# One hybrid decoder layer: the weight stream packed by the host, q, k and v computed together per k-tile

## The chip, the cores and the metric

The kernel runs on one core of one Trainium2 chip. Engines: PE (TensorE) multiplies and transposes, PEld is its weight load, DVE is VectorE, ACT is ScalarE, POOL is GpSimd, SP only issues transfers here. The metric is device time in microseconds (us), lower is better; the time of a kernel is the median of its runs. Packing the inputs is done by the host before the launch and is not in the time.

## The reference

One layer with two parallel mixers on 256 positions of width 1024, one batch, all float32. Cut to what matters:

```python
proj = x @ w_in                       # 1024 -> 512 q, 512 k, 512 v, 512 B, 512 C, 512 h, 2048 gates
q, k = partial_rope(q), partial_rope(k)            # first 16 of 64 dims of each of 8 heads
y_att = causal_softmax_attention(q, k, v) @ w_attn_out   # one block of 256: plain causal attention
y_cnv = (B * causal_dwconv3(C * h, conv_w_mix)) @ w_conv_out
g_att, g_cnv = sigmoid(gates + b_gate)             # 1024 each
mix = (g_att * y_att + g_cnv * y_cnv) @ w_o
x = layer_norm(2 ** 0.25 * x + mix, ln1)
u = causal_dwconv3(x @ w_up, conv_w_ffn)           # 1024 -> 5632
f = (silu(u[:, :2816]) * u[:, 2816:]) @ w_down     # 2816 -> 1024
x = layer_norm(2 ** 0.25 * x + f, ln2)
```

## The kernel before

**Three products for one.** Every float32 operand is split into a high part h, rounded to a type that PE takes in one pass, and the rest l = value - h. A product is then h*h + h*l + l*h, three matmuls (`mm3`, L295; `passes`, L465). A split (`hl_split`, L194) is one ACT copy that makes h (L195) and one DVE subtraction that makes l (L196). Both activations and all weights go through it. Below, a *pass* is one matmul with 512 moving columns.

**The weight stream.** All weights, 16.0 million numbers, come from memory in chunks of 1 MB, each of one tile `raw` of 128 x 2048; there are three such tiles (`RAW_BUFS`). The list of chunks is made first: `add_chunk` (L82) notes the transfers of a chunk and its *units*, the pieces that are split at once, two to a chunk, 128 x 1024 numbers each. `issue_dma` (L168) issues, all on SP's queue (L174), the transfers up to two chunks beyond the one whose split begins. A split unit lies in a pair of tiles `wh`, `wl`; there are nine of each (`HL_BUFS`). `ahead(u)` (L323) splits four units (`LA`) beyond the one that PE is about to use. A chunk of w_in or w_up columns is read as 8 x 128 rows of 1 KB, q, k and v chunks as rows of 2 KB, chunks of whole rows of w_o and w_down as rows of 4 KB.

**The order.** The program is in order on each engine, as written. Work that belongs beside the stream is hung on units: `at(u, f)` (L429) puts f after unit u's matmuls, `run(u)` (L432) emits what hangs there.

- *Start.* `warm_up` runs 20 and later 8 matmuls on zeros. x (`xr`, 128 positions on the partitions, two tiles) comes in five pieces between the pieces of the first two chunks. PE transposes it, 16 blocks of 128 x 128 (`x_transpose`, L244), and a split of each result from PSUM gives `xT`: x with the model dimension on the partitions, eight *k-tiles* of 128. Small constants (convolution taps, gate bias) come by five transfers on POOL's queue, as rows; two PE transposes (`small_consts`, L255) and two ACT copies bring them into columns.
- *q, k, v* (L498), one after the other, each over all eight k-tiles, two PSUM banks each (positions 0 to 127 and 128 to 255): 3 x 8 x 2 x 3 = 144 passes. q's first k-tiles are interleaved by hand with the arrival of x (`first_unit`, L473). Rope (`rope`, L337, eight DVE instructions) hangs on the first unit of v, the transposes of q and k (`qk_transpose`) on v's last unit and the first unit after it.
- *conv and gates* (L541 to L571): 12 units of h, C and B and 16 of gates, each 24 matmuls with 256 moving columns (`unit_cols`, L310). Call the first of these units C0 and count from it. Attention hangs on them for four pairs of heads p: `scores` at C0+1+3p, `masked` (mask, maximum; DVE), `exps` (ACT), `normalize` (DVE) one unit later each; `probs_T` (six transposes into two banks) at C0+6+5p, then `probs_hl` twice (split of the probabilities), `attend`, `attend_hl` (split of the attention output; it empties attend's bank).
- *rest*: the output products and gating, w_o, layer norm with x as residual (L624), the FFN with its convolution, w_down, layer norm.

PSUM's eight banks are two rings of four. `acc_bank` holds the accumulators of q, k, v, conv, gates and down; `ps_bank` holds transposes, scores and attend. A bank is given out again in the order of the ring as soon as its last reader is done.

Of the kernel before, what the change touches and what calls it, by code (L numbers as in the profile page):

```python
# [8 lines left out]
F32 = mybir.dt.float32  # L9
# [39 lines left out]

@with_exitstack  # L50
def layer_kernel(ctx: ExitStack, tc: tile.TileContext, x, positions, w_in, b_gate, w_attn_out,
                 conv_w_mix, w_conv_out, w_o, ln1_g, ln1_b, w_up, conv_w_ffn, w_down,
                 ln2_g, ln2_b, out):
    nc = tc.nc
    w_in, w_ao, w_co, w_o, w_up, w_dn = (w[0] for w in (w_in, w_attn_out, w_conv_out, w_o, w_up, w_down))
# [21 lines left out]
    WARM = (20, 8)  # L77
    units = []
    dmas = []
    state = {"dma": 0}  # L80

    def add_chunk(loads, views):  # L82

        c = len(dmas)
        dmas.append(dict(loads=loads, tile=None))
        for v in views:
            units.append(dict(chunk=c, view=v, h=None, l=None))

    def kxn(w, k0, k1, c0, c1):
        return w[k0 * P:k1 * P, c0:c1].rearrange("(k p) n -> p k n", p=P)  # L90

    def chunk_cols(w, c0, order=None):
        add_chunk([(lambda t: t.rearrange("p (k n) -> p k n", k=8), kxn(w, 0, 8, c0, c0 + 256))],
                  [(lambda t, u=u: t.rearrange("p (k n) -> p k n", k=8)[:, :, u * P:(u + 1) * P], [8, P])
                   for u in range(2)] if order is None else order)

    U = {}

    def mark(name):
        U[name] = len(units)  # L100


    def x_load(k0, k1):
        return (lambda t: xr[:, :, k0 * P:k1 * P], x[0, :, k0 * P:k1 * P].rearrange("(t p) d -> p t d", p=P))

    def k_load(c, k0, k1):
        return (lambda t: t.rearrange("p (k n) -> p k n", k=4)[:, k0:k1, :],
                kxn(w_in, c * 4 + k0, c * 4 + k1, 0, 512))

    for i, nm in enumerate("qkv"):  # L110
        mark(nm)
        for half in range(2):
            loads = [(lambda t: t.rearrange("p (k n) -> p k n", k=4),
                      kxn(w_in, half * 4, half * 4 + 4, i * 512, i * 512 + 512))]
            if i == 0 and half == 0:
                loads = [x_load(0, 1), k_load(0, 0, 1), x_load(1, 2), k_load(0, 1, 2), x_load(2, 4), k_load(0, 2, 3), k_load(0, 3, 4)]
            elif i == 0:
                loads = [x_load(4, 6), k_load(1, 0, 1), k_load(1, 1, 2), x_load(6, 8), k_load(1, 2, 4)]
            add_chunk(loads, [(lambda t, u=u: t.rearrange("p (k n) -> p k n", k=4)[:, 2 * u:2 * u + 2, :], [2, 512])
                              for u in range(2)])  # L120

    OFF_B, OFF_C, OFF_H, OFF_G = 3 * AW, 3 * AW + CW, 3 * AW + 2 * CW, 3 * AW + 3 * CW
    for pr in range(2):
        for off in (OFF_H, OFF_C, OFF_B):
            U[(off, pr)] = len(units)
            chunk_cols(w_in, off + pr * 256)
    for pr in range(8):
        U[("g", pr)] = len(units)
        chunk_cols(w_in, OFF_G + pr * 256)

    for half in range(2):
        for nm, w in (("ao", w_ao), ("co", w_co)):
            U[(nm, half)] = len(units)
            add_chunk([(lambda t: t.rearrange("p (k n) -> p k n", k=4), kxn(w, 0, 4, half * 512, half * 512 + 512))],
                      [(lambda t, u=u: t.rearrange("p (k n) -> p k n", k=4)[:, :, u * 256:(u + 1) * 256], [4, 256])
                       for u in range(2)])

    def row_chunk(w, k):
        add_chunk([(lambda t: t.rearrange("p (k n) -> p k n", k=2), kxn(w, k, k + 2, 0, D))],
                  [(lambda t, u=u: t.rearrange("p (k n) -> p k n", k=2)[:, u:u + 1, :], [1, D]) for u in range(2)])  # L140

    mark("wo")
    for k in range(0, 8, 2):
        row_chunk(w_o, k)

    mark("up0")
    for half in range(2):
        add_chunk([(lambda t: t.rearrange("p (k n) -> p k n", k=4)[:, :, 0:256], kxn(w_up, half * 4, half * 4 + 4, 0, 256)),
                   (lambda t: t.rearrange("p (k n) -> p k n", k=4)[:, :, 256:512],
                    kxn(w_up, half * 4, half * 4 + 4, DFF, DFF + 256))],  # L150
                  [(lambda t, u=u: t.rearrange("p (k n) -> p k n", k=4)[:, 2 * u:2 * u + 2, :], [2, 512])
                   for u in range(2)])
    TAIL = 8
    for c in range(1, NP // 2):
        U[("ug", c)] = len(units)
        chunk_cols(w_up, c * 256)
        U[("uv", c)] = len(units)
        chunk_cols(w_up, DFF + c * 256)
        d = c - 2
        if 0 <= 2 * d < NP - TAIL:  # L160
            U[("dn", d)] = len(units)
            row_chunk(w_dn, 2 * d)
    for d in range((NP - TAIL) // 2, NP // 2):
        if ("dn", d) not in U:
            U[("dn", d)] = len(units)
            row_chunk(w_dn, 2 * d)

    def issue_dma(c):  # L168
        while state["dma"] <= c and state["dma"] < len(dmas):
            d = dmas[state["dma"]]  # L170
            t = wp.tile([P, 2048], F32, tag="raw", name=f"raw{state['dma']}", bufs=RAW_BUFS)
            d["tile"] = t
            for fn, src in d["loads"]:
                nc.sync.dma_start(fn(t), src)  # L174
            state["dma"] += 1

    def split_start(u):
        un = units[u]
        issue_dma(un["chunk"] + RAW_BUFS - 1)
        k, n = un["view"][1]  # L180
        un["h"] = wp.tile([P, k, n], F32R, tag="wh", name=f"wh{u}", bufs=HL_BUFS)
        un["l"] = wp.tile([P, k, n], F32R, tag="wl", name=f"wl{u}", bufs=HL_BUFS)

    def split_part(u, k0, k1, eng=None):
        un = units[u]
        src = un["view"][0](dmas[un["chunk"]]["tile"])
        hl_split(un["h"][:, k0:k1], un["l"][:, k0:k1], src[:, k0:k1], eng)

    def split(u, eng=None):
        if u < len(units) and units[u]["h"] is None:  # L190
            split_start(u)
            split_part(u, 0, units[u]["view"][1][0], eng)
# [18 lines left out]

    warm_up(WARM[0])

# [16 lines left out]
    nc.gpsimd.dma_start(posi, positions[0].rearrange("(t p) -> p t", p=P))  # L230
    rowsA = cst.tile([116, P], F32, name="rowsA")
    cf = conv_w_ffn[0].rearrange("t (j p) -> t j p", p=P)
    nc.gpsimd.dma_start(rowsA[0:44], cf[0])
    nc.gpsimd.dma_start(rowsA[44:88], cf[1])
    nc.gpsimd.dma_start(rowsA[88:104], b_gate[0].rearrange("(j p) -> j p", p=P))
    nc.gpsimd.dma_start(rowsA[104:116], conv_w_mix[0].rearrange("t (j p) -> (t j) p", p=P))
    rowsB = cst.tile([44, P], F32, name="rowsB")
    nc.gpsimd.dma_start(rowsB, cf[2])
# [5 lines left out]
    def x_transpose(k0, k1):  # L244
        b = ps_bank(f"xt{k0}")
        for k in range(k0, k1):
            for t in range(2):
                nc.tensor.transpose(b[:, (k - k0) * 256 + t * P:(k - k0) * 256 + (t + 1) * P],
                                    xr[:, t, k * P:(k + 1) * P], ident)
        hl_split(xh[:, k0:k1, :], xl[:, k0:k1, :], b[:, 0:(k1 - k0) * 256].rearrange("p (j t) -> p j t", j=k1 - k0))  # L250

    cA = cst.tile([P, 116], F32, name="cA")
    cB = cst.tile([P, 44], F32, name="cB")

    def small_consts():  # L255
        b = ps_bank("cst")
        nc.tensor.transpose(b[:, 0:116], rowsA, ident[:116, :116])
        nc.tensor.transpose(b[:, 128:172], rowsB, ident[:44, :44])
        nc.scalar.activation(cA, b[:, 0:116], AF.Copy)
        nc.scalar.activation(cB, b[:, 128:172], AF.Copy)  # L260

    def w_ffn(tap, j):
        return cB[:, j:j + 1] if tap == 2 else cA[:, tap * 44 + j:tap * 44 + j + 1]

    def bias_gate(j):
        return cA[:, 88 + j:89 + j]

    def w_mix(tap, j):
        return cA[:, 104 + tap * 4 + j:105 + tap * 4 + j]
# [31 lines left out]
    def unit_rows(u, k0, banks, ah, al, first, last, ts=(0, 1)):  # L301

        un = units[u]
        nk = un["view"][1][0]
# [5 lines left out]
    def unit_cols(u, o, bh, bl, n0=0):  # L310

        un = units[u]
        nk = un["view"][1][0]
# [137 lines left out]
    C0 = U[(OFF_H, 0)]  # L451
    for p in range(4):
        s = C0 + 1 + 3 * p
# [434 lines left out]
```

## Time and profile before

| | |
|---|---|
| time, median of 3 runs | 380.79 us (379.37, 381.06, 380.79) |
| the profiled execution | 378.92 us, of which its span 377.1 us |
| granted PE clock, mean over the span | 0.993 |
| stages on PE, from the chain | q to 19.8, k to 30.9, v to 41.8, conv and gates from there |
| DMA | 68.65 MB, mean 182 GB/s over the span |
| SP's queue | 66.07 MB in 48992 packets |

The span runs from the first to the last instruction. A row of the timeline has start, duration, engine, line, operation, output <- input and count, with the idle time before it and who ended it in brackets. A row of the chain has start, duration, engine, output, line and count. A row of waits has the waiting engine and line, whom it waited for, the total, the count and the longest. A row of groups has the shape, the count, the busy time and the mean ns of one, then the idle time before. A row of windows has the stretch, its length, the busy time and count of PE, PEld, DVE, ACT and POOL, then granted clock, DMA share and GB/s. A row of transfers has the count, the size in units of 1024 bytes and the us to landing. A matmul's duration contains its pipeline: matmuls follow each other faster than they last.

### The profile page before, as it was taken

How to read it: one execution, taken by the hardware profiler on the slowest of the kernel's cores; microseconds unless marked ns; L12 is line 12 of the kernel's file. 1: busy time of each engine (PE TensorE's matmuls, PEld its weight loads, DVE VectorE, ACT ScalarE, POOL GpSimd, SP SyncE). 2: the span in 40 equal slices, each digit the busy share in tenths (PEclk: the TensorE clock that was granted, in tenths of full speed). 3: DMA queues.
4: the chain of work that ended last, by engine and by line, in shares of the span. 5: the costliest groups of instructions: out<-in, count | busy, mean ns of one | idle time of the engine just before them, and what ended most of it. 6: DMA issues, size and time to landing. Idle time of an engine off the chain costs nothing.

```text
span 377.1 us, 6375 instructions
## 1 busy us (share of the span) xinstructions
PE 367.1 (97%) x2582; PEld 342.4 (91%) x2582; DVE 273.1 (72%) x455; ACT 200.5 (53%) x325; POOL 12.6 (3%) x33
## 2 busy tenths in 40 slices
PE   7999999999999999999999999999999999999991
PEld 6888999999999999988899999999999999999891
DVE  2777777778536458879879876958769687678584
ACT  4667485648655545544167563646546555466200
POOL 5000000000000000102100000000000000000012
PEclk9999999999999999999999999999999999999997
DMA  7996764444644445497451919365493765660011
GB/s 214 370 320 216 227 197 139 130 139 164 211 139 159 177 143 194 140 345 245 163 196 43 314 28 312 114 224 175 160 318 106 249 220 170 228 237 38 2 56 56
DMA packets 49789, 68.65 MB, mean 182 GB/s; under 512 B 1431, under 2 KB 40032, under 8 KB 49760
## 3 DMA queue, kind: packets, MB, share of 16 engines
q1 hardware_dynamic: 48992, 66.07, 51.9%
q0 software_dynamic: 768, 2.18, 1.7%
q8 instruction: 20, 0.33, 0.4%
q14 instruction: 9, 0.07, 0.1%
HBM read 67.19 MB, written 1.05 MB: 181 GB/s over the span
## 4 chain that ended last, share of the span: by engine, by line
PE 96%; DMA 1%; DVE 1%; SPq 0%; issue 0%; DVEq 0%
PE pb L318 10%; PE pb L317 10%; PE pb L316 10%; PE d L298 5%; PE d L297 5%; PE d L299 5%; PE g L317 4%; PE g L316 4%; PE g L318 4%; PE q L470 3%; PE y L318 2%; PE y L317 2%; PE y L316 2%; PE o L297 2%; PE o L299 2%; PE o L298 2%
## 5 line engine op out<-in xcount | busy, mean ns | idle before, releaser
L196 DVE TENSOR_TENSOR wl<-raw,wh 128x1024 fp32r<-128x1024 f32 (+1 forms) x126 | 148.2, 1188 | 55.3 <-ACT wh L195 53.4
L195 ACT ACTIVATE wh<-raw 128x1024 fp32r<-128x1024 f32 (+1 forms) x126 | 127.1, 1025 | 48.8 <-DMA raw<-in_w_up 33.1
L316 PE MATMUL pb<-x1T,wh 128*128 128x256 f32 x320 | 90.6, 283 | 0.0
L318 PE MATMUL pb<-x1T,wl 128*128 128x256 f32 x320 | 90.6, 283 | 0.0
L317 PE MATMUL pb<-x1T,wh 128*128 128x256 f32 x320 | 90.5, 283 | 0.0
L317 PEld LDWEIGHTS pb<-x1T,wh 128*128 128x128 f32 x320 | 61.4, 192 | 0.6
L316 PEld LDWEIGHTS pb<-x1T,wh 128*128 128x128 f32 x320 | 61.4, 192 | 0.6
L318 PEld LDWEIGHTS pb<-x1T,wl 128*128 128x128 f32 x320 | 61.4, 192 | 0.0
L316 PE MATMUL g<-xT,wh 128*128 128x256 f32 x128 | 36.5, 285 | 0.0
L318 PE MATMUL g<-xT,wl 128*128 128x256 f32 x128 | 36.2, 283 | 0.0
L317 PE MATMUL g<-xT,wh 128*128 128x256 f32 x128 | 36.2, 283 | 0.0
L297 PE MATMUL d<-wh,f 128*128 128x512 f32 x80 | 31.3, 391 | 0.0
L298 PE MATMUL d<-wl,f 128*128 128x512 f32 x80 | 31.3, 391 | 0.0
L299 PE MATMUL d<-wh,f 128*128 128x512 f32 x80 | 31.1, 389 | 0.0
L694 DVE SCALAR_TENSOR_TENSOR fc<-pb,cA,fc 128x255 f32<-128x255 f32 x44 | 21.0, 477 | 7.2 <-ACT fc L690 7.2
L317 PEld LDWEIGHTS g<-xT,wh 128*128 128x128 f32 x128 | 24.5, 192 | 0.0
L316 PEld LDWEIGHTS g<-xT,wh 128*128 128x128 f32 x128 | 24.5, 192 | 0.0
L318 PEld LDWEIGHTS g<-xT,wl 128*128 128x128 f32 x128 | 24.5, 192 | 0.0
L690 ACT ACTIVATE fc<-pb,cB 128x256 f32<-128x256 f32 x44 | 18.2, 464 | 10.2 <-PE pb L318 8.4
L696 DVE SCALAR_TENSOR_TENSOR fc<-pb,cA,fc 128x254 f32<-128x254 f32 x44 | 21.2, 482 | 1.6
L299 PEld LDWEIGHTS d<-wh,f 128*128 128x128 f32 x80 | 15.0, 188 | 3.2
L297 PEld LDWEIGHTS d<-wh,f 128*128 128x128 f32 x80 | 15.1, 188 | 2.7
(193 smaller groups left out, 665.8 us busy)
## 6 DMA issues: line engine op xcount, KB each, us to landing
raw<-in_w_up SPq DMA_DIRECT2D x20, 1024.0 KB, 5.6
raw<-in_w_in SPq DMA_DIRECT2D x18, 1024.0 KB, 5.2
raw<-in_w_down SPq DMA_DIRECT2D x11, 1024.0 KB, 6.9
raw<-in_w_o SPq DMA_DIRECT2D x4, 1024.0 KB, 4.8
raw<-in_w_attn_out SPq DMA_DIRECT2D x2, 1024.0 KB, 4.9
raw<-in_w_conv_out SPq DMA_DIRECT2D x2, 1024.0 KB, 4.8
raw<-in_w_up SPq DMA_DIRECT2D x4, 512.0 KB, 6.5
raw<-in_w_in SPq DMA_DIRECT2D x6, 256.0 KB, 5.5
```

Source lines behind the costliest of these rows:

```text
L195: nc.scalar.activation(h, src, AF.Copy)
L196: (eng or nc.vector).tensor_tensor(l, src, h.bitcast(F32), op=ALU.subtract)
L297: nc.tensor.matmul(o, ah, bh, start=start, stop=False)
L298: nc.tensor.matmul(o, ah, bl, start=False, stop=False)
L299: nc.tensor.matmul(o, al, bh, start=False, stop=stop)
L316: nc.tensor.matmul(o, wh, bh[:, k, :], start=k == 0, stop=False)
L317: nc.tensor.matmul(o, wh, bl[:, k, :], start=False, stop=False)
L318: nc.tensor.matmul(o, wl, bh[:, k, :], start=False, stop=k == nk - 1)
L470: nc.tensor.matmul(banks[t], x2[p == 2], un["l" if p == 1 else "h"][:, k, :], start=start and p == 0, stop=stop and p == 2)
L690: nc.scalar.activation(c, pb[:, a * S:(a + 1) * S], AF.Copy, scale=w_ffn(2, j))
L694: nc.vector.scalar_tensor_tensor(c[:, 1:S], pb[:, a * S:a * S + S - 1], w_ffn(1, j), c[:, 1:S], op0=ALU.mult, op1=ALU.add)
L696: nc.vector.scalar_tensor_tensor(c[:, 2:S], pb[:, a * S:a * S + S - 2], w_ffn(0, j), c[:, 2:S], op0=ALU.mult, op1=ALU.add)
```

## The change

The host packs all weights, and x transposed, into one array `wpack` of chunks x 128 x 2048 in the order of use (`packed`, `plan`), so that a chunk of 1 MB is 128 rows of 8 KB. The first eight chunks are new: chunk k holds k-tile k of x transposed (256 columns), of w_in's q and k columns (1024, one unit) and of its v columns (512, one unit), 1792 columns or 917 KB. Chunks behind these have the same contents and the same split units as before. `cpack` is the small constants in columns, 128 x 160.

- x_transpose, small_consts and their copies and splits go; x comes split from `raw` (`x_split`), the constants come by one transfer.
- q, k and v are computed k-tile by k-tile (`qkv_passes`): per k-tile 18 passes into six banks, v's two from `ps_bank`.
- Chunk 0 comes in four pieces (x on ACT's queue, q, k and v on SP's), chunk 1 in two, all others in one.
- k-tile 0 is split in part on DVE alone (x and the q half: copy and subtraction), the rest on ACT and DVE. All later k-tiles are split two k-tiles ahead.
- 36 warm-ups in one group, in place of 20 and 8.
- The first four conv units are split during k-tiles 6 and 7.
- Rope moves behind C0, qk_transpose behind C0+2 and C0+3, scores to C0+4+3p, probs_T to C0+9+4p, the rest with them. Conv and gates stay.
- x for the residual (`xr`, 1 MB) comes in one transfer on SP's queue behind chunk 20.

The core of the diff:

```diff
+    mark("qkv")
+    for k in range(KT):
+        chunk((1, S, [("xT", k, k + 1, 0, S)]),
+              (2, 512, [("w_in", k, k + 1, 0, 1024)]),
+              (1, 512, [("w_in", k, k + 1, 1024, 1536)]))
...
+    PIECES = {0: (0, 256, 768, 1280, 1792), 1: (0, 768, 1792)}
+    XR_CHUNK = 20
     def issue_dma(c):
...
+            cuts = PIECES.get(i, (0, end))
+            for a, b in zip(cuts, cuts[1:]):
+                (nc.scalar if i == b - 256 == 0 else nc.sync).dma_start(t[:, a:b], wpack[i, :, a:b])
+            if i == XR_CHUNK:
+                nc.sync.dma_start(xr, x[0].rearrange("(t p) d -> p t d", p=P))
...
-    warm_up(WARM[0])
+    warm_up(36)
...
+    consts = cst.tile([P, 160], F32, name="consts")
+    nc.gpsimd.dma_start(consts, cpack)
...
-    at(3, small_consts)
-    at(5, rope_tables)
-    at(U["v"], rope, 0)
-    at(U["v"], rope, 1)
+    at(C0, rope, 0)
+    at(C0, rope, 1)
     for i, g2 in enumerate((0, 2, 1, 3)):
-        at(U["v"] + 3 + i // 2, qk_transpose, g2)
+        at(C0 + 2 + i // 2, qk_transpose, g2)
     for p in range(4):
-        s = C0 + 1 + 3 * p
+        s = C0 + 4 + 3 * p
...
-        s = C0 + 6 + 5 * p
+        s = C0 + 9 + 4 * p
...
+    def x_split(k):
+        issue_dma(k + RAW_BUFS - 1)
+        hl_split(xh[:, k, :], xl[:, k, :], raws[k][:, 0:S])
+    def qkv_split(k):
+        if k < KT:
+            x_split(k)
+            split(U["qkv"] + 3 * k + 1)
+            split(U["qkv"] + 3 * k + 2)
...
+    banks = [[acc_bank(f"{m}{t}") for t in range(2)] for m in "qk"] + [[ps_bank(f"v{t}") for t in range(2)]]
+    def qkv_passes(k, m, ts, ps):
+        wh, wl = qkv_weights(k, m)
+        for t in ts:
+            for p in ps:
+                nc.tensor.matmul(banks[m][t], (xl if p == 2 else xh)[:, k, t * P:(t + 1) * P], wl if p == 1 else wh,
+                                 start=k == 0 and p == 0, stop=k == KT - 1 and p == 2)
+    split_start(1)
+    issue_dma(RAW_BUFS - 1)
+    nc.vector.tensor_copy(xh[:, 0, :], raws[0][:, 0:S])
+    nc.vector.tensor_tensor(xl[:, 0, :], raws[0][:, 0:S], xh[:, 0, :].bitcast(F32), op=ALU.subtract)
+    w0, wh0, wl0 = raw_of(1), units[1]["h"], units[1]["l"]
+    nc.vector.tensor_copy(wh0[:, 0], w0[:, 0])
+    qkv_passes(0, 0, (0, 1), (0, 2))
+    nc.vector.tensor_tensor(wl0[:, 0], w0[:, 0], wh0[:, 0].bitcast(F32), op=ALU.subtract)
+    qkv_passes(0, 0, (0, 1), (1,))
+    split_part(1, 1, 2)
+    qkv_passes(0, 1, (0, 1), (0, 2, 1))
+    split(2)
+    qkv_passes(0, 2, (0, 1), (0, 2, 1))
+    qkv_split(1)
+    qkv_split(2)
+    for k in range(1, KT):
+        for m in range(3):
+            if k >= KT - 2 and m < 2:
+                split(C0 + 2 * (k - KT + 2) + m)
+            qkv_passes(k, m, (0, 1), (0, 1, 2))
+            if k == KT - 1:
+                if m < 2:
+                    evac_rows(m, banks[m])
+                else:
+                    evac_v(banks[m])
+        qkv_split(k + 2)
+        if k == 2:
+            rope_tables()
+    cur["u"] = C0 + 4
```

More of the change, by code (lines that the diff above doesn't have):

```diff
@@ L50, in layer_kernel @@
 @with_exitstack
-def layer_kernel(ctx: ExitStack, tc: tile.TileContext, x, positions, w_in, b_gate, w_attn_out,
-                 conv_w_mix, w_conv_out, w_o, ln1_g, ln1_b, w_up, conv_w_ffn, w_down,
-                 ln2_g, ln2_b, out):
+def layer_kernel(ctx: ExitStack, tc: tile.TileContext, x, positions, wpack, cpack, ln1_g, ln1_b, ln2_g, ln2_b, out):
     nc = tc.nc
-    w_in, w_ao, w_co, w_o, w_up, w_dn = (w[0] for w in (w_in, w_attn_out, w_conv_out, w_o, w_up, w_down))
     cst = ctx.enter_context(tc.tile_pool(name="cst", bufs=1))
@@ L76, in layer_kernel @@
     RAW_BUFS, HL_BUFS = 3, 9
[L77 to L166, printed above, removed]
-    def issue_dma(c):
[L169 to L175, printed above, removed]
+    chunks, plan_units, U = plan()
@@ new lines, in layer_kernel @@
+    units = [dict(chunk=c, off=off, shape=(k, n), h=None, l=None) for c, off, k, n, _ in plan_units]
+    raws = []
+    PIECES = {0: (0, 256, 768, 1280, 1792), 1: (0, 768, 1792)}
+    XR_CHUNK = 20
+    def issue_dma(c):
+        while len(raws) <= c and len(raws) < len(chunks):
+            i = len(raws)
+            t = wp.tile([P, CHUNK], F32, tag="raw", name=f"raw{i}", bufs=RAW_BUFS)
+            raws.append(t)
+            last = units[chunks[i][-1]]
+            end = last["off"] + last["shape"][0] * last["shape"][1]
+            cuts = PIECES.get(i, (0, end))
[3 more added lines that the diff above has]
+                nc.sync.dma_start(xr, x[0].rearrange("(t p) d -> p t d", p=P))
@@ L179, in split_start, with raw_of @@
         issue_dma(un["chunk"] + RAW_BUFS - 1)
-        k, n = un["view"][1]
+        k, n = un["shape"]
         un["h"] = wp.tile([P, k, n], F32R, tag="wh", name=f"wh{u}", bufs=HL_BUFS)
         un["l"] = wp.tile([P, k, n], F32R, tag="wl", name=f"wl{u}", bufs=HL_BUFS)
+    def raw_of(u):
+        un = units[u]
+        k, n = un["shape"]
+        return raws[un["chunk"]][:, un["off"]:un["off"] + k * n].rearrange("p (k n) -> p k n", k=k)
     def split_part(u, k0, k1, eng=None):
         un = units[u]
-        src = un["view"][0](dmas[un["chunk"]]["tile"])
-        hl_split(un["h"][:, k0:k1], un["l"][:, k0:k1], src[:, k0:k1], eng)
+        hl_split(un["h"][:, k0:k1], un["l"][:, k0:k1], raw_of(u)[:, k0:k1], eng)
     def split(u, eng=None):
@@ L191, in split @@
             split_start(u)
-            split_part(u, 0, units[u]["view"][1][0], eng)
+            split_part(u, 0, units[u]["shape"][0], eng)
     def hl_split(h, l, src, eng=None):
@@ L303, in unit_rows @@
         un = units[u]
-        nk = un["view"][1][0]
+        nk = un["shape"][0]
         for t in ts:
@@ L463, in layer_kernel, with qkv_weights @@
         at(s + 4, attend_hl, p)
-    def passes(c, k, banks, ts, ps, start=False, stop=False):
-        un = units[c]
+    def x_split(k):
[6 more added lines that the diff above has]
+            split(U["qkv"] + 3 * k + 2)
+    def qkv_weights(k, m):
+        ua, ub = (units[U["qkv"] + 3 * k + 1 + e] for e in range(2))
+        return (ub["h"][:, 0, :], ub["l"][:, 0, :]) if m == 2 else (ua["h"][:, m, :], ua["l"][:, m, :])
```

154 lines of the change are left out of this document (78 added, 76 removed).

## The prediction

> **What bounds the kernel now.** I read the busy table and the heads of the chain first.
>
> ```profile
> span 377.1 us, 6375 instructions
> PE 367.1 (97%) x2582; PEld 342.4 (91%) x2582; DVE 273.1 (72%) x455; ACT 200.5 (53%) x325; POOL 12.6 (3%) x33
> PE 96%; DMA 1%; DVE 1%; SPq 0%; issue 0%; DVEq 0%
> ```
>
> PE is the bound, on 96% of the chain. The view of waits, for PE alone, has only three rows, and I set one row of ACT's beside them:
>
> ```profile
> PE warm L210 <- DVE zeros L200: 1.0, 1, 1.0
> PE xt L248 <- DMA xr<-in_x: 0.8, 1, 0.8
> PE q L470 <- ACT wh L195: 0.5, 1, 0.5
> ACT wh L195 <- DMA raw<-in_w_up: 33.1, 16, 3.4
> ```
>
> All three of PE's waits lie in the first 8 us. ACT waits 33.1 us for streamed weights in the FFN, yet none of this reaches PE: the splits run four units ahead. So time can come from two places only, work taken off PE and the start. The chain in order of time shows the start:
>
> ```profile
> 7.86 0.66 PE xt L248 x4
> 8.52 1.84 PE q L470 x8
> 10.36 0.50 PE xt L248 x4
> 10.86 2.76 PE q L470 x12
> 13.62 0.44 PE xt L248 x4
> 14.05 5.50 PE q L470 x24
> 19.84 0.43 PE k L297
> ...
> 41.83 0.87 PE qkt L354 x8
> ```
>
> From 7.86 us on PE never stops. The k and v stages are 96 passes (matmuls of 512 columns) between 19.84 and 41.83, so 0.229 us for one. Of q's 48 passes 8 + 12 + 24 = 44 stand behind 7.86, so 140 passes of q, k and v: 140 x 0.229 = 32.07. Between them lie 12 of the 16 transposes of x (0.66 + 0.50 + 0.44 = 1.60) and, from 19.55 to 19.84, the two transposes of the constants (0.29). 7.86 + 32.07 + 1.60 + 0.29 = 41.82: the stage is accounted for. Its end, 41.83, is what I predict anew. After it PE has the same matmuls in both kernels.
>
> **The change, part by part.**
>
> *Transposes gone.* The 12 on the chain and the two of the constants: 1.60 + 0.29 = 1.89 us of PE, off the path. The other four lie in the start, which is reckoned anew.
>
> *The first k-tile.* It needs the warm-ups, x's first piece and the q piece. For these and the next step:
>
> ```profile
> 0.74 0.43 SPq L174 DMA_DIRECT2D xr<-in_x  x1
> 0.99 2.05 PEld L210 LDWEIGHTS <-zeros 128*128 128x128 bf16 x20 [0.99 <-DVE zeros L200]
> 1.24 0.45 SPq L174 DMA_DIRECT2D raw<-in_w_in  x1
> 4.36 0.63 ACT L195 ACTIVATE wh<-raw 128x512 fp32r<-128x512 f32 x1 [0.21 <-DMA raw<-in_w_in]
> 5.04 1.22 PE L470 MATMUL q<-wh,xT 128*128 128x512 f32 x2 [0.46 <-ACT wh L195]
> 2.00:8.00 6.00, 4.78 (x30) 3.72 (x28) 1.84 (x4) 2.04 (x5) 4.11 (x17) 1.00 0.91 251
> 8.00:12.00 4.00, 4.00 (x22) 3.26 (x22) 2.76 (x5) 2.75 (x6) 0.00 (x0) 1.00 1.03 353
> 2.00:3.00 1.00, 1.00 (x13) 1.00 (x10) 0.00 (x0) 0.03 (x1) 0.99 (x12) 1.00 0.97 216
> 3.00:4.00 1.00, 1.00 (x10) 0.93 (x9) 0.00 (x0) 0.23 (x1) 1.00 (x2) 1.00 0.94 311
> L196 DVE TENSOR_TENSOR wl<-raw,wh 128x1024 fp32r<-128x1024 f32 x13 | 15.4, 1222 | 4.9 <-ACT wh L195 4.8
> L195 ACT ACTIVATE wh<-raw 128x1024 fp32r<-128x1024 f32 x13 | 13.0, 1054 | 2.4 <-DMA raw<-in_w_in 2.4
> L196 DVE TENSOR_TENSOR wl<-raw,wh 128x512 fp32r<-128x512 f32 x8 | 5.2, 686 | 0.6 <-ACT wh L195 0.6
> L195 ACT ACTIVATE wh<-raw 128x512 fp32r<-128x512 f32 x8 | 4.7, 625 | 0.2 <-DMA raw<-in_w_in 0.2
> L196 DVE TENSOR_TENSOR xT<-xt,xT 128x256 fp32r<-128x256 f32 x2 | 0.8, 425 | 4.6 <-ACT xT L195 4.6
> L195 ACT ACTIVATE xT<-xt 128x256 fp32r<-128x256 f32 x2 | 0.8, 384 | 3.4 <-PE xt L248 3.4
> ```
>
> The 36 warm-ups at 2.05 / 20 = 0.103 us run from 0.99 to 4.7; I put 4.8. The old first weight piece, 262 KB, was issued at 1.24 and read at 4.36, so 3.1 us; the q piece, the same size and first on its queue at 0.74, is due by 3.9, and x's 131 KB on ACT's queue sooner. A DVE copy of 512 has no row: at most the subtraction's 0.69, at least the 0.42 of half the length. So the first weights are ready at 4.3 to 4.6, behind the warm-ups. First pass: 4.8, against 5.04. The two passes at 5.04 took 1.22, 0.6 each, where settled ones are 0.229 apart; with the first three at 0.4 and 15 at 0.229 the 18 passes of k-tile 0 end at 4.8 + 1.2 + 3.4 = 9.4.
>
> *The second k-tile.* New and decisive: its q and k weights are one unit of 1024 columns, split by one ACT instruction that waits for both pieces of chunk 1. Ahead of that landing the queues carry 131 + 3 x 262 + 393 + 524 = 1835 KB and 82 KB of constants, 1917 KB. Slow bound: the old kernel's own pace, 16 KB by 2 us, then 251 GB/s to 8 us (1506 KB) and 353 for the other 395 KB: 9.1 us. Fast bound: 353 GB/s from 2.0 on: 7.4. I take 216 and 311 GB/s for 2 to 4 us, then 353, so 4 + (1917 - 16 - 527) / 353 = 7.9, because the old queue mixed x's short rows and five small POOL transfers into 4 to 8 us, while the new pieces are rows of 2 KB and more. With 0.2 until ACT starts: wh from 8.1 to 9.15 (1054 ns), wl to 10.4 (1222 ns). The second pass of k-tile 1 needs wl, so PE waits from about 9.6 to 10.4. From there 125 of the 144 passes are left: 10.4 + 125 x 0.229 = 39.0. k-tile 2 is 917 KB behind: at 353 GB/s 2.6 us later, 10.7, split by 0.38 + 1.05 + 1.22 at about 13.6, and PE arrives at 10.4 + 17 x 0.229 = 14.3. Each later one gains 4.1 - 2.6 us.
>
> Term one: 41.83 - 39.0 = **2.8 us less** (1.89 of transposes, 0.9 of start); bounds 9.1 and 7.4 us for the landing give 1.6 and 3.3.
>
> *Six banks.* v's two come from the other pool; q and k are emptied while v's passes run (6 x 0.229 = 1.4 us against two copies near 0.6). Nothing.
>
> *Conv units split early.* Four splits of 1.05 and 1.22 move into k-tiles 6 and 7, where 18 passes take 4.1 us and ACT has 0.38 + 1.05 + 0.63 of its own. Nothing; without that cover, 1.2 us at the first conv unit.
>
> *Rope and attention later.* Rope, eight DVE instructions, sits behind v's two subtractions and one split, its reader three units later. Scores, softmax and transposes of probabilities follow three units later than before, and after the first pair at a step of 4, not 5. Here a wait is new. The score banks of pair 3 (the scores now stand right behind attend_hl(0) and probs_T(1)) include the bank that attend(0) filled, so the second matmul of these scores waits until DVE has emptied it; everything on PE stands behind. Before, that bank went to the next transposes, a unit later. Rows:
>
> ```profile
> 50.20 0.32 PE c L316
> 59.03 0.89 PE s L369 x12
> L532 DVE SCALAR_TENSOR_TENSOR ct<-z,cA,ct 128x256 f32<-128x256 f32 x8 | 3.7, 482 | 0.1
> L196 DVE TENSOR_TENSOR aT<-av,aT 64x256 fp32r<-64x256 f32 x8 | 3.4, 422 | 6.6 <-ACT aT L195 6.4
> L377 DVE CUSTOM_DVE_ANT_0 sm<-s,mask 128x256 f32<-128x256 f32 x8 | 3.1, 421 | 0.0
> L377 DVE CUSTOM_DVE_ANT_0 sm<-s,mask 128x128 f32<-128x128 f32 x8 | 2.0, 287 | 1.2 <-PE s L369 1.2
> 80.00:85.00 5.00, 5.00 (x48) 4.79 (x47) 4.86 (x18) 2.46 (x6) 0.00 (x0) 1.00 0.34 97
> ```
>
> Three units take 59.03 - 50.20 = 8.83 us. From the end of scores(2) PE needs 8.83, attend's 1.0 (3 x 0.23 + 3 x 0.12) and six transposes (0.87 / 8 each, 0.65): 10.5 us. DVE meanwhile: mask 1.4 (2 x 0.42 + 2 x 0.29), conv taps 4 x 0.48, a split 1.22, the product 0.69, yT 0.63 (ACT) and 0.69, a split 1.22, twice aT 0.38 (ACT) and 0.42: 9.4 us, and 2.6 us in front (z 0.69, a split 1.22, vpt at most 0.69) as far as not done earlier. So between 1.1 us of slack and 1.5 us of wait; I take 0.2 of wait, the middle. The order of gates and exponentials also costs ACT two more table loads; gate banks are needed again four units, 11.8 us, later. Nothing.
>
> *Stream laid out by the host, x late.* Rows of 1 KB become 8 KB. The issues by line show what row length does:
>
> ```profile
> raw<-in_w_in SPq DMA_DIRECT2D x18, 1024.0 KB, 5.2
> raw<-in_w_down SPq DMA_DIRECT2D x11, 1024.0 KB, 6.9
> ```
>
> w_down's rows of 4 KB land in 6.9 us, the w_in chunks, mostly rows of 1 KB, in 5.2: no gain from length, and no wait of PE's to shorten. x's 1 MB now goes into SP's queue behind chunk 20, during the gates; the chunk behind it comes some 3 us later (1049 KB at 353), covered by splits 11.8 us ahead. Without cover, 3 us. The four POOL transfers fewer are worth nothing beyond the start.
>
> A rule of the Trainium skill goes further ("DMA: Bandwidth & Descriptors", Rules for kernel authors: for full bandwidth, 128 partitions and at least 1 MiB per transfer, small ones merged). By it larger transfers would be worth something wherever data is awaited, here at the start alone; the two rows above, both of 1 MB, cannot show it.
>
> **Sum.** 2.8 - 0.2 = 2.6 us less, span 374.5. The profiled execution took 378.92 (span 377.1 and 1.82 around it), 1.87 below the median of the runs, 380.79; with its own surroundings it would be 376.3. Against the median: **378.2 us**; its own range, from the landing, 377.6 to 379.0.
>
> **The rivals.**
>
> *The start is slow as before* (21%). If 251 GB/s belongs to the first microseconds and not to the short rows, chunk 1 lands at 9.1, wl is ready at 11.6 and the stage ends at 40.2: gain 1.6 - 0.2 = 1.4, 379.4 us. For it: 4.78 of 6 us PE busy and DMA at a share of 0.91 in that row, so the engines were not idle. Against: 311 GB/s at 3 to 4 us.
>
> *The stream is at full pace at once* (10%). Landing at 7.4, wl at 9.9, end 38.5, no ring wait: gain 3.3, 377.5 us. The Trainium skill's rule above leans this way. Against: 216 GB/s at 2 to 3 us with 2 KB rows already among them.
>
> *The bank wait decides* (11%, slower). One place: pair 3's scores behind attend_hl(0). If DVE is a further 3.5 us late when it comes to the mask of pair 2, the wait is 1.5 + 3.5 = 5.0, and 380.79 - 2.8 + 5.0 = 383.0 us. It ends above the old time from a wait of 2.8 us on. For it: DVE at 4.86 of 5 us in 80 to 85, and the attention now denser. Against: PE is at 5.00 in that same row, and DVE has spare time before.
>
> *The host's layout brings nothing*: already in the sum, at zero.
>
> **How the numbers follow.** A measurement of this kernel cannot tell less than about 0.5%, 1.9 us, from no change (its runs lie 1.7 apart); the line for faster is 378.9. Forecast 58%, of which 5 points end above that line. Faster: 53 + 10 = 63%. Same: 5 + 21 = 26%. Slower: 11%. Range 376.7 to 380.5: the fast start less 0.8 of scatter, the slow start with nearly the whole 1.5 of bank wait in place of 0.2, 1.1 more.
>
> **What would show it.** In the changed kernel's profile: no matmuls of x's transposes; first q pass near 4.8; one PE wait on k-tile 1's weights, near 0.8 us, ended by ACT's wh or DVE's wl; the first conv matmul near 39.0; a PE wait of at most 1.5 us at pair 3's scores; no other wait of PE's; PE rates of 0.229 and 2.94 / 24 us unchanged. Wrong would be: waits at k-tile 2 or later, a wait for raw during the FFN, or a longer matmul step.

## The result and the profile after

| | before | changed |
|---|---|---|
| median of 5 runs | 380.79 us (379.37 to 381.83) | 377.76 us (377.59 to 377.95) |
| ratio of the runs | 1 | 0.9945 (95% interval 0.9923 to 0.9967) |
| profiled execution, span | 378.92, 377.1 | 377.95, 376.2 |
| first matmul after v, start | 41.67 us | 40.45 us |

The changed kernel is faster by 0.55% by this ratio and by 0.80% by the two medians: the ratio is not formed from the medians, whose quotient, 377.76 / 380.79, is 0.9920. Three figures do not fit together with one cause: the medians lie 3.0 us apart, the two profiled executions only 1.0, and the old runs are spread over 2.5 us, the new ones over 0.4. Most of the experiments are about that.

The page of the changed kernel begins:

```profile
span 376.2 us, 6359 instructions
PE 366.5 (97%) x2572; PEld 342.6 (91%) x2572; DVE 273.7 (73%) x461; ACT 203.4 (54%) x327; POOL 10.3 (3%) x29
```

PE is still the bound. Its waits (waiting engine and line, whom it waited for, total, count, longest) are two, where there were three:

```profile
PE warm L202 <- DVE zeros L192: 1.0, 1, 1.0
PE q L451 <- DVE wh L460: 0.6, 1, 0.6
```

So nothing behind the first pass waited in this execution, neither at k-tile 1 nor at the scores of pair 3. The chain in order of time (start, duration, what) shows the start:

```profile
0.74 3.71 DMA raw<-in_wpack
4.47 0.30 DVE xT L457
4.80 0.43 DVE xT L458
5.22 0.35 DVE wh L460
5.61 2.93 PE q L451 x6
8.54 2.13 PE k L451 x6
10.67 1.38 PE v L451 x6
12.05 1.36 PE q L451 x6
...
39.25 1.36 PE v L451 x6
```

These rows show two rates of the same instruction. From 12.05 on six passes take 1.36 us, 0.227 each, as later everywhere. The first six took 2.93 and the next 2.13: k-tile 0 took 6.44 us instead of 4.08. And x, issued at 0.74, was read at 4.47, 1.5 us after the old kernel's first piece of the same size (issued at 0.74, read at 3.00). The timeline shows when k-tile 1 was ready (start, duration, engine, line, operation, count, idle time before):

```profile
9.07 1.58 ACT L187 ACTIVATE wh<-raw 128x1024 fp32r<-128x1024 f32 x2 [1.13 <-DMA raw<-in_wpack]
...
10.16 1.83 DVE L188 TENSOR_TENSOR wl<-raw,wh 128x1024 fp32r<-128x1024 f32 x2 [1.76 <-ACT wh L187]
```

Chunk 1's second piece was read at 9.07, and with 1.2 us for its subtraction wl was ready at 11.4. PE came at 11.9, late enough by its own slowness not to wait. Everything behind follows 1.2 us earlier than before: the first matmul after v starts at 40.45 instead of 41.67, and the last DVE instruction at 371.61 instead of 372.84. Between these two points both kernels take the same time, 331.16 and 331.17 us, so in the two profiles the whole gain lies in the start. Of the 1.23, 0.3 is lost after the last DVE instruction, where only the output transfers are left; what they waited for was not tried.

### The profile page after: what moved, and what is told of

Its sections match the earlier page's. It is cut to its first block, busy times and chain, and to the rows that moved or that the text cites. A ratio compares the mean times of both kernels' runs of the same rounds, so it can differ in the third digit from the quotient of the medians.

```text
span 376.2 us, 6359 instructions
## 1 busy us (share of the span) xinstructions
PE 366.5 (97%) x2572; PEld 342.6 (91%) x2572; DVE 273.7 (73%) x461; ACT 203.4 (54%) x327; POOL 10.3 (3%) x29
## 4 chain that ended last, share of the span: by engine, by line
PE 96%; DVE 1%; DMA 1%; issue 0%; DVEq 0%
PE pb L286 10%; PE pb L285 10%; PE pb L284 10%; PE d L265 5%; PE d L266 5%; PE d L267 5%; PE g L284 4%; PE g L286 4%; PE g L285 4%; PE q L451 3%; PE k L451 3%; PE v L451 3%; PE y L286 2%; PE y L285 2%; PE y L284 2%; PE o L266 2%
## 5 line engine op out<-in xcount | busy, mean ns | idle before, releaser
L188 DVE TENSOR_TENSOR wl<-raw,wh 128x1024 fp32r<-128x1024 f32 (+1 forms) x126 | 147.5, 1183 | 50.3 <-ACT wh L187 47.8
L187 ACT ACTIVATE wh<-raw 128x1024 fp32r<-128x1024 f32 (+1 forms) x126 | 126.9, 1023 | 43.3 <-DMA raw<-in_wpack 34.9
L665 DVE SCALAR_TENSOR_TENSOR fc<-pb,consts,fc 128x255 f32<-128x255 f32 x44 | 20.9, 476 | 13.9 <-ACT fc L661 13.9
L661 ACT ACTIVATE fc<-pb,consts 128x256 f32<-128x256 f32 x44 | 18.3, 468 | 18.5 <-PE pb L286 16.6
L667 DVE SCALAR_TENSOR_TENSOR fc<-pb,consts,fc 128x254 f32<-128x254 f32 x44 | 21.2, 481 | 1.6
```

The source lines that it names most:

```text
L187: nc.scalar.activation(h, src, AF.Copy)
L188: (eng or nc.vector).tensor_tensor(l, src, h.bitcast(F32), op=ALU.subtract)
L661: nc.scalar.activation(c, pb[:, a * S:(a + 1) * S], AF.Copy, scale=w_ffn(2, j))
L665: nc.vector.scalar_tensor_tensor(c[:, 1:S], pb[:, a * S:a * S + S - 1], w_ffn(1, j), c[:, 1:S], op0=ALU.mult, op1=ALU.add)
L667: nc.vector.scalar_tensor_tensor(c[:, 2:S], pb[:, a * S:a * S + S - 2], w_ffn(0, j), c[:, 2:S], op0=ALU.mult, op1=ALU.add)
```

## The experiments

All were run against the kernel before on the same chip. Each has 5 to 12 runs, and those of the kernel before, 30, 17 and 18 on three chips, have medians of 379.8, 380.2 and 379.8 us. All of these lie below the 380.79 of the five runs above.

**The kernel before once more** (no edit).

> The kernel before, unchanged, to see how much of the 3.0 us between the two medians (380.79 and 377.76) lies in its own scatter: its first profile had a span of 377.1, only 0.9 above the changed kernel's 376.2. Theory 'path' (the start of the old kernel is the same each time): this profile again ends v at 41.8 and has a span of 376.8 to 377.5. Rival 'moving start' (the moment from which a 512-column pass takes 0.23 us instead of 0.43, and the landings of x, differ from execution to execution): v ends 0.5 to 2.5 us elsewhere, with the difference all before 15 us, and the times spread over 2 us again while the changed kernel's spread over 0.4.

379.28 us median (378.88 to 382.64, 12 runs); the profiled execution, 380.91, had a span of 379.1, and the first matmul after v started at 43.66, 2.0 later than in its first profile. One of PE's waits:

```profile
PE xt L248 <- DMA xr<-in_x: 2.2, 1, 2.2
```

and PE's timeline behind it:

```profile
8.53 1.12 PE L248 MATMUL xt<-ident,xr 128*128 128x128 f32 x4 [2.22 <-DMA xr<-in_x]
...
9.88 1.05 PE L470 MATMUL q<-wh,xT 128*128 128x512 f32 x2
...
11.79 0.40 PE L470 MATMUL q<-wl,xT 128*128 128x512 f32 x1
```

The wait for x's third piece was 2.2 us in place of 0.8, and after it passes ran 0.42 apart until about 11.6. The windows (length, busy times, then granted clock, DMA share, GB/s) name the reason:

```profile
9.00:10.00 1.00, 1.00 (x6) 0.90 (x5) 0.00 (x0) 0.31 (x1) 0.00 (x0) 0.50 1.09 400
10.00:11.00 1.00, 1.00 (x4) 0.81 (x3) 0.68 (x2) 1.00 (x3) 0.00 (x0) 0.50 1.05 384
```

The granted clock was 0.50. "Moving start" held: the old kernel loses time twice in such an execution, by the late piece and by the half clock behind the gap. The Trainium skill ("TensorE: Matmul & The Clock Gate", Part 1: The HAM clock gate) puts such a fall to half rate after at least one idle window of some 3.4 us, and says that the windows run free. The trace agrees in the half, 0.50, and in a fall during an idle stretch, but this stretch was 2.2 us, shorter than the page's window; here the measurement decides.

**Filling that wait.** The granted clock may fall because PE is idle, or the late piece alone may matter.

```diff
             passes(c, 0, banks, (0,), (1, 2))
+            warm_up(16)
             x_transpose(2, 4)
```

> The kernel before with 16 warm-up matmuls more, just ahead of the transposes that wait for x's third piece; the granted clock fell to 0.50 in its second profile after a wait of 2.2 us there, and passes ran 0.42 apart until 11.6. Theory 'gap' (the clock falls because PE is idle): with the wait filled the runs above 380.5 become rare, the best runs stay at 378.8 to 379.6 (the filling costs up to 0.9 us where x is on time), mean clock 0.99 or more in every run. Rival 'only the landing' (x is late, the clock is a side effect): the scatter to 381 and 382 stays.

Runs in order, us and mean granted clock of the span:

```
before, same chip: 378.67 .994  379.19 .996  379.32 .996  379.35 .996  379.43 .996  379.49 .993  379.50 .997  379.51 .994  379.74 .992
                   379.91 .995  380.05 .996  380.75 .988  380.79 .988  381.02 .988  381.09 .988  381.09 .989  381.11 .989  382.23 .986
filled:            378.82 .993  379.03 .994  379.05 .994  379.25 .996  379.27 .996  379.27 .996  379.42 .996  379.46 .993  379.97 .994
                   380.31 .995  380.41 .995  380.58 .995
```

"Gap" held. Unfilled, 7 of 18 runs lie at 380.7 or above, each with a mean clock below 0.99; filled, no run of 12 has such a clock and one reaches 380.5. The profiled execution, at 380.31 one of the slower ones, shows a full clock where 0.50 had been granted:

```profile
9.00:10.00 1.00, 1.00 (x11) 1.00 (x9) 0.00 (x0) 0.00 (x0) 0.00 (x0) 1.00 1.06 390
```

Median 379.35 against 379.83, ratio 0.9988 (0.9972 to 1.0004): what is won in the bad runs is not enough to be certain in the median, but no run of that class was seen again. The class is a part of the old median that one profile alone does not show. It is not all of the scatter: on the other two chips 14 of 47 runs of the kernel before have such a clock, but six more lie at 380.9 to 382.2 with a clock of 0.992 to 0.994. No trace of such a run was taken, and what slows them stays open.

**The transposes alone.** x transposed and the constants in columns come from the host; x for the residual is therefore loaded later, and nothing else changes.

```diff
-                nc.tensor.transpose(b[:, (k - k0) * 256 + t * P:(k - k0) * 256 + (t + 1) * P],
-                                    xr[:, t, k * P:(k + 1) * P], ident)
-        hl_split(xh[:, k0:k1, :], xl[:, k0:k1, :], b[:, 0:(k1 - k0) * 256].rearrange("p (j t) -> p j t", j=k1 - k0))
+        hl_split(xh[:, k0:k1, :], xl[:, k0:k1, :], xraw[:, k0:k1, :])
...
-    at(3, small_consts)
```

> The kernel before with one part of the change alone: x transposed and the constants in columns come from the host, so that PE's 18 transposes and their five PSUM splits go; x for the residual is loaded later. Order of q, k, v, pieces, warm-ups and attention stay. Theory 'path': the 12 transposes on the chain (1.60) and the two of the constants (0.29) fall away and q's start keeps its waits for data: the stage ends 1.9 to 2.5 us earlier than 41.8, so nearly the whole gain of the change is here. Rival 'start decides' (the first passes wait for data and run slowly, so that work taken off PE turns into waiting): less than 1 us.

378.56 us (378.12 to 379.50, 12 runs), ratio 0.9958 (0.9939 to 0.9976): 1.2 us less in the median, 0.7 in the best run, and no run above 379.5. Its profiled execution (379.06, not one of its best) has these waits of PE:

```profile
PE q L452 <- ACT wh L199: 2.8, 3, 1.3
PE q L452 <- DVE wl L200: 0.4, 2, 0.2
```

The median lies between the two theories, as "path" asked for 1.9 to 2.5 us and "start decides" for less than 1; the best run goes with the second. In this execution the 1.89 us of transposes on PE became waiting. PE waited 3.2 us for q's weights, in five places up to 11.66, where the old profile has 0.8 and 0.5 behind the warm-ups, and the first matmul after v started at 41.87, no earlier than before. The median won all the same, and the scatter is gone already here: no run of 12 has a mean clock below 0.993.

In that order q alone asks for 393 KB (x and weights) per 6 passes, 1.36 us of PE, which is 289 GB/s, when the old kernel's queues moved, from 2 to 8 us, 251 and 233 GB/s in its two profiles and 223 here (the changed kernel's 315). Six banks ask for 917 KB per 18 passes, 4.08 us: 225 GB/s. This is a reason to expect something of the order by k-tiles, but that order was not run alone. The changed kernel lies 0.7 to 0.8 us below this run's median, on other chips, and the order shares that with the warm-ups, the pieces and the later attention.

**The layout alone.** All chunks contiguous in memory, with the pieces, the order and the transposes as before.

```diff
-        dmas.append(dict(loads=loads, tile=None))
+        dmas.append(dict(loads=loads if c < 2 else [(lambda t: t, wpack[c])], tile=None))
...
-        return (lambda t: t.rearrange("p (k n) -> p k n", k=4)[:, k0:k1, :],
-                kxn(w_in, c * 4 + k0, c * 4 + k1, 0, 512))
+        return (lambda t: t[:, k0 * 512:k1 * 512], wpack[c, :, k0 * 512:k1 * 512])
```

> The kernel before with the host's layout alone: every chunk's tile is 128 contiguous rows of 8 KB in memory; the same units, pieces of the first two chunks, order and transposes. Theory 'nobody waits for the stream' (after 8 us PE never waits): best run within 0.4 us of the kernel before's best, 378.8, median within 0.6, and scatter as before. Rival 'the stream's layout is worth something': 1 us or more less, in the best run as in the median. In between: the start's pieces land sooner and the scatter shrinks.

380.29 us (379.59 to 380.94, 12 runs) against 380.23, ratio 0.9999 (0.9981 to 1.0017). Nothing in the median, as reckoned. The scatter was narrower on both sides, and the best run was 0.6 us worse than the other's best, 378.97, where at most 0.4 had been expected; in the profiled execution q's first weights were read at 4.97 instead of 4.36. Why is not known.

**x early.** `XR_CHUNK = 20` becomes 2.

> The changed kernel with x for the residual (1 MB) behind chunk 2 instead of chunk 20, so ahead of chunk 3 on SP's queue. Chunk 3 and those after it land 2.5 to 3 us later (1.05 MB at 350 to 420 GB/s). In the changed kernel k-tile 3 is read at 13.4 and reached by PE at 20.2, with 2.7 us of splitting between: 4 us of spare time. Theory 'covered': the same time within 0.3 us. Rival 'x late is part of the gain' (the stream has no such reserve in the first 20 us): PE waits at k-tile 3 or 4 and 0.5 to 3 us are lost.

377.72 us (377.55 to 378.15, 6 runs); the changed kernel itself on that chip took 377.84. "Covered" held: a megabyte ahead of chunk 3 costs nothing.

**The changed kernel once more** (no edit).

> The changed kernel, unchanged, beside the variants on the same chip. 'Steady start' (it reaches its first weights late and runs them slowly, but without a gap of PE's behind them): 377.5 to 378.0 in all runs, first pass 5.4 to 5.8, fast steps of 0.227 from 9 to 10 us, the kernel before scattered from 378.8 to 382. 'Chance' (the few runs seen were alike by accident): times up to 379 or more.

377.84 us (377.38 to 378.19, 6 runs), ratio 0.9927 (0.9899 to 0.9955). The narrow spread held, a little wider than the 377.5 to 378.0 expected, but the reason given for it did not. This execution started quickly:

```profile
5.69 1.21 PE L451 MATMUL q<-wh,xT 128*128 128x512 f32 x4 [1.02 <-DVE wh L460]
...
10.40 0.50 PE L451 MATMUL q<-wh,xT 128*128 128x512 f32 x1 [0.30 <-ACT wh L187]
...
11.66 0.50 PE L451 MATMUL q<-wl,xT 128*128 128x512 f32 x1 [0.76 <-DVE wl L188]
```

Four passes took 1.21 us instead of 2.08; PE then reached k-tile 1 at 10.1 and waited 1.06 us for it. The first matmul after v started at 40.14, against 40.45. So the changed kernel has two bounds that lie close together: slow passes until 9.6, or wl of k-tile 1 at 11.3 to 11.7. Whichever of the two ways an execution started, it ended within 0.3 us of the other (spans 376.2 and 375.9).

**More warm-ups.** `warm_up(36)` becomes 44.

> The changed kernel with 44 warm-ups in place of 36, which at 0.107 us each end near 5.7 instead of 4.8 and so cover the 0.6 us in which PE waits for the first weights. In the changed kernel the first 9 passes start 0.43 us apart, until about 9.6, instead of 0.227. Theory 'activity' (PE is slow until it has been busy without a gap for long enough): the fast steps begin 1 to 3 us earlier, k-tile 0 ends near 10.5 instead of 12.05, k-tile 1 then waits for wl (ready near 11.4), and the stage ends 0.5 to 0.9 us earlier. Rival 'fixed moment' (the fast steps begin at a moment that does not hang on the gap): they begin at 9.6 again, or anywhere, and the time is the same within 0.3 us. Trainium skill, 'TensorE: Matmul & The Clock Gate', section on the clock gate: a free-running window of 3.4 us must be busy; by that the gap may or may not fall into the deciding window.

377.58 us (377.31 to 377.95, 7 runs); fast passes from the first on (5.86), then 0.77 us of waiting for wl, first matmul after v at 39.76. Two of PE's waits:

```profile
PE q L451 <- DVE wh L460: 0.9, 1, 0.9
PE q L451 <- DVE wl L188: 0.8, 1, 0.8
```

The stage ended 0.7 us before that of the first profile, as "activity" had it, and the median lies 0.2 to 0.3 below those of the changed kernel (on other chips), as its rival had it: k-tile 1 is the next bound. The wait for the first weights was not covered, it was 0.9 us. The warm-ups had become faster while they ran: 10 of their weight loads lie between 4.0 and 4.5 us, 6 between 1.0 and 1.5, and all 44 were done by 4.95. In the changed kernel's first profile, where the first passes were slow, it was 6 or 7 in every half microsecond until the 36 were done. So this trace does not show that a start without a gap is what counts, and the same fast start was seen above with 36.

**k-tile 1 in halves.** Its unit of q and k is split by two ACT and two DVE instructions, q's first, so that q waits for the first piece of chunk 1 only. With 44 warm-ups and with 36:

```diff
             x_split(k)
-            split(U["qkv"] + 3 * k + 1)
+            if k == 1:
+                u = U["qkv"] + 3 * k + 1
+                split_start(u)
+                split_part(u, 0, 1)
+                split_part(u, 1, 2)
+            else:
+                split(U["qkv"] + 3 * k + 1)
```

> The changed kernel with 44 warm-ups, and k-tile 1's unit of q and k split in two halves (one ACT and one DVE instruction each for q and for k), so that its q passes wait for the first piece of chunk 1 (read at 7.5 in the changed kernel) and not for the second (read at 9.07). Theory 'the start bounds': with 44 warm-ups the first passes are fast and PE then waits 0.77 us for k-tile 1's wl; with the halves q's wl is ready at 9.2 to 9.5, k's at 10.4, v's at 11.0, k-tile 0 ends at 9.9 to 10.1, so the wait falls to 0.3 or less and the stage ends near 38.9 instead of 40.6: 1.4 to 1.8 us less than the changed kernel, 376.0 to 376.4. Rival 'landing of all of chunk 1 or 2 bounds': the wait moves to v of k-tile 1 or to k-tile 2, and 0.7 us or less is won.

> The changed kernel with k-tile 1's unit in two halves but its own 36 warm-ups. Two profiles of the changed kernel took two ways to the same end: in one the first nine passes were slow (0.43 us apart, to 9.6), PE came to k-tile 1 at 11.89 and waited for nothing; in the other all were fast and PE waited 1.06 us for k-tile 1. Theory 'two bounds' (either the slow passes or the landing): with the halves alone executions that start fast come to 375.9 to 376.5 as with 44 warm-ups, those that start slowly to 377.4 to 378.0, so the times split or lie between. Rival 'the halves are enough': all at 376.0 to 376.5. Rival 'the warm-ups did it': all at 377.5 to 378.2.

With 44: **375.96 us** (375.95 to 376.46, 5 runs), ratio 0.9881 (0.9853 to 0.9908) to the kernel before and 1.9 us under the changed kernel on the same chip. PE's waits, all there are:

```profile
PE warm L202 <- DVE zeros L192: 1.0, 1, 1.0
PE q L457 <- DVE wh L466: 0.7, 1, 0.7
```

and the timeline at k-tile 1:

```profile
7.79 0.62 ACT L187 ACTIVATE wh<-raw 128x512 fp32r<-128x512 f32 x1
...
8.44 0.69 DVE L188 TENSOR_TENSOR wl<-raw,wh 128x512 fp32r<-128x512 f32 x1
...
10.13 0.39 PE L457 MATMUL q<-wh,xT 128*128 128x512 f32 x1
...
10.35 0.39 PE L457 MATMUL q<-wl,xT 128*128 128x512 f32 x1
```

q's wl is there at 9.1 and PE comes at 10.13: no wait. The first matmul after v starts at 38.69. Here too the 44 warm-ups left a wait for the first weights, 0.7 us, and the first passes were fast. With 36 warm-ups the runs split, as "two bounds" had it, into two groups and nothing between: 375.92, 375.98, 376.04 and 377.72, 377.96, 378.05, 378.19. Its profiled execution is of the second kind (four passes at 5.61 in 2.08 us, first matmul after v at 40.52). Neither edit wins alone: 44 warm-ups bring 0.2 to 0.3 us (measured on another chip), halves win in only three of 7 runs, both together bring 1.9 us in the median and at least 1.4 in each of five runs. Five against three of 7, on two chips, speaks for the warm-ups but is not many; by chance alone, at three in 7, five such runs in a row would come up about once in 70 (an estimate from these counts).

**x on SP's queue.** Alone, and with the halves and 40 warm-ups:

```diff
-                (nc.scalar if i == b - 256 == 0 else nc.sync).dma_start(t[:, a:b], wpack[i, :, a:b])
+                nc.sync.dma_start(t[:, a:b], wpack[i, :, a:b])
```

> The changed kernel with x's first piece on SP's queue, ahead of the q piece, in place of ACT's queue. In the changed kernel x's 131 KB, issued at 0.74, were read at 4.47; in the kernel before the first 131 KB on SP's queue, issued at 0.74, were read at 3.0. Theory 'shared' (the two queues take turns, so x ends with the q and k pieces): x is read at 3.0 to 3.3, the q piece at 4.2 to 4.5, the first pass at 4.8 to 5.0 instead of 5.61, and the stage of q, k and v ends 0.3 to 0.8 us earlier. Rival 'start-up' (the first bytes of any queue come late): x is read at 4.2 or later and the q piece 0.5 later still, the first pass is at 5.6 to 6.2, and nothing is won or up to 0.5 us lost.

> Halves, x's first piece on SP's queue ahead of the q piece, and 40 warm-ups (to 5.3). With x on SP's queue alone the first pass was at 5.10, but five of 12 runs took 379.2 to 380.1. Theory 'gap' (those runs came from PE waiting for k-tile 1 long enough to fall back to slow passes; the halves take that wait away): first pass at 5.1 to 5.4, stage end 0.3 to 0.6 us before that of the halves with 44 warm-ups, 375.4 to 376.0, no run above 377. Rival 'one queue is itself unsteady' (the q piece lands late in some executions): runs of 377.5 and more remain.

Alone: 378.28 us (377.18 to 380.09, 12 runs). The timeline of DVE and PE:

```profile
3.20 0.29 DVE L457 CAST xT<-raw 128x256 fp32r<-128x256 f32 x1 [2.27 <-DMA raw<-in_wpack]
...
4.62 0.43 DVE L460 CAST wh<-raw 128x512 fp32r<-128x512 f32 x1 [0.66 <-DMA raw<-in_wpack]
...
10.29 0.19 PEld L451 LDWEIGHTS q<-wh,xT 128*128 128x128 f32 x1 [0.33 <-ACT wh L187]
...
11.55 0.50 PE L451 MATMUL q<-wl,xT 128*128 128x512 f32 x1 [0.77 <-DVE wl L188]
```

"Shared" is right on the order of arrival: x is read at 3.20 instead of 4.47, the first pass starts at 5.10. On the second queue x comes late; that it then takes turns with the q and k pieces fits, but was not measured apart. The best runs gained a little, the median did not: five of 12 runs took 379.2 to 380.1, with mean clocks of 0.990 to 0.991 against 0.992 to 0.996 in the others. With the halves no run exceeds 377.05: 376.12 us (375.92 to 377.05, 6 runs), ratio 0.9904 (0.9882 to 0.9926). The bad runs went when the wait at k-tile 1 was broken up, which speaks for "gap" again; but the warm-ups changed with it, and that the clock fell there was not seen in a trace, since the profiled execution of the version without halves was a good one. The forecast of 375.4 to 376.0 was too low. In the profiled execution, the slowest of the six, PE came to k-tile 1 sooner, at 9.30, and waited 0.7 us for wl, in three parts:

```profile
PE q L457 <- DVE wl L188: 0.7, 3, 0.3
```

## Why the prediction was right, and where it was not

The time, 377.76, is 0.4 from the 378.2 forecast and in the likeliest case's own range. That it came so near is luck: two errors nearly cancel.

- **The 2.6 us were reckoned from one profiled execution (378.92) and taken off the median of the runs (380.79).** This is the step that failed most. The old median contains runs whose start goes worse than in that profile (43.66 instead of 41.67 for the first matmul after v), and no run of the changed kernel, 11 in all, lies above 378.19. Of the 3.0 us between the medians the two profiles show 1.0. They understate it, since the old one is better than any of the five old runs and the new one the slowest of its five; the best runs lie 1.8 apart here and 1.6 on the chip where both kernels ran again. The rest is scatter that is gone, and chance: the old median came from five runs, and where it came from 17 the two medians are 2.4 apart (380.23 and 377.84).
- **Term one, 2.8 us, was 1.2.** The landing of chunk 1 had been put at 7.9, within 7.4 to 9.1; it was read at 9.07, at the slow bound. The pace had been put well enough: a mean of 16 GB/s to 2 us and 315 from 2 to 8 make 1922 KB by 8.0, the 1917 KB of the sum. By 9.07, with 436 GB/s from 8 to 9, the queues had moved some 2390 KB. So the sum was wrong in letting chunk 1 be there as soon as that many bytes had moved; where the last microsecond went, the traces, which give no times by DMA engine, do not show. The rival with the slow start ended the stage at 40.2; 40.14 and 40.45 were measured. In its end that rival came true, but not in its cause, a pace of 251 GB/s. And in the first profile the landing did not bind at all: k-tile 0, put at 9.4, lasted until 11.9 by its slow passes.

  ```profile
  2.00:8.00 6.00, 5.40 (x35) 4.65 (x33) 2.98 (x7) 2.14 (x4) 1.87 (x13) 1.00 0.92 315
  ```

- **The transposes, 1.89 us.** They are gone from PE, but alone they gave 1.2 in the median and 0.7 in the best run, and in the profiled execution all of it became waiting. The sum had them on a path that was, in those microseconds, in part the stream's.
- **First pass at 4.8.** It was at 5.61. x on ACT's queue "sooner" than the q piece at 3.9 was wrong: it was read at 4.47, and at 3.20 on SP's queue. The copy of 512 columns took 0.42, its lower bound.
- **Three slow passes.** Nine in one profile, none in another. What 36 warm-ups do to the clock at the first pass is not settled by them; 44 started fast in both profiles and, with the halves, left no slow group in the times.
- **The wait at pair 3's scores.** None: attend's bank was empty at 87.0 and the scores came at 88.15, so 1.1 us of slack, the one end of what the sum had between 1.1 of slack and 1.5 of wait.

  ```profile
  86.58 0.43 DVE L188 TENSOR_TENSOR aT<-av,aT 64x256 fp32r<-64x256 f32 x1 [0.45 <-ACT aT L187]
  ...
  88.15 0.95 PE L337 MATMUL s<-qkT 64*128 64x128 f32 x12
  ```

- **Costed at nothing**, and found so: the layout (0.9999 alone), x late (377.72 against 377.84), six banks, conv splits, rope and the table loads (no wait of PE's). The Trainium skill's rule on large transfers ("DMA: Bandwidth & Descriptors", Rules for kernel authors) finds no support in the layout run; its transfers were as large before, so it is not refuted either.

## What to carry to other kernels

When the old kernel's runs scatter by more than the gain in question, look for where a second profile differs from the first before reckoning: a mechanism that removes scatter moves the median without moving the best profile. Removing work from the bound engine is worth its full price only where that engine, not the stream, sets the pace; in the first ten microseconds ask how many bytes a microsecond of matmul needs. Two bounds that lie within half a microsecond of each other hide each other: only both edits together (warm-ups and the split of the awaited unit) brought the gain in every run. And a median of a few scattered runs is itself a chance: here five gave 380.79, and 17 to 30 gave 379.8 to 380.2.

## What was not expected of the hardware

In one trace a wait of 2.2 us in the start was enough for the granted clock to fall to 0.50 for some 3 us. More than a third of the old kernel's runs on one chip share the low mean clock of that execution (7 of 18 below 0.99). The 0.6 to 1.0 us waits in the changed kernel's two traces did not do this, and its mean clock was 0.992 or more in all runs. Passes 0.43 us apart at the very start stand in windows whose granted clock is printed as 1.00. The same distance, 0.42, goes with a printed 0.50 in the old kernel's second profile, and 0.227 with 1.00 later on, so at the start the distance of the passes says more than the column. And 131 KB on a queue of its own were read 1.3 us later than the same bytes at the head of the shared queue.
